# The sample's products over 64 rows made over 128, with zeros in the upper rows

## The chip, the cores and the metric

The kernel runs on one core of a Trainium2 chip. The core has five instruction queues that matter here: TensorE (PE, with its weight loads PEld), VectorE (DVE), ScalarE (ACT), GpSimd (POOL) and SyncE (SP, which issues the DMAs). Each queue runs in the order in which its instructions were written; semaphores hold an instruction back until what it reads is there. The metric is the device time of one execution in microseconds. A profile comes from one further execution.

## The reference

One layer of a streaming encoder for two inputs: a prompt of 2048 new frames, and a sample of 64 frames that continues a running stream. Half of the layer's columns go to attention in chunks (8 heads of 64), the other half to a gated linear recurrence (4 heads of 128). Cut to what matters:

```
xn = rms_norm(h) ; aq, ak, av, ag, hq, hf, hi, hg = split(xn @ w_in)
# attention of the sample: 512 cached keys and its own 64
p = softmax(q @ concat(cache_k, k).T * scale + bias) ; o = p @ concat(cache_v, v)
# recurrence, in blocks, per head (S: 128 x 128)
A = where(mask, q~ @ k~.T, 0) ; o = q~ @ S + A @ v ; S = exp(bl) * S + (k * exp(bl - b)).T @ v
y = h + concat(o_attn * silu(ag), rms_norm(o_rec) * silu(hg)) @ w_out ; rms_norm(y)
```

For the sample the sums over keys (the last 64 of 576) and over frames in a block (64) have 64 terms, where all others have 128.

## The kernel before

All inputs are float32. The prompt is worked through in four stages of 512 frames ("super-blocks"); the second stage has 576 columns, the 64 extra ones being the sample. In each stage PE makes 32 projections of 128 output columns (the products "acc", 24 wide steps each, since operands are split into a high and a low part), and between them the small products of attention and recurrence. The second stage lies at about 260 to 600 us of the span; its projections are cut into 256 and 320 columns.

The tiles that matter: v holds nine blocks of 128 keys for a pair of attention heads; the sample's values are the first 64 rows of block 8. ph holds transposed softmax weights (two buffers). gi (in the code iv) holds the recurrence's values, five blocks of 128 frames, the sample's in block 4. k1 (shown as "k", in the code kn) holds transposed keys. asb (A) holds masked scores. So is the sample's state. wraw serves as the cache's keys and values in this stage.

For the sample three products have 64 rows (frames or keys) on the array's contraction side: in sample_a the last of five products of each head into pv, with ph and v; in rec_block the product kv (kn with iv, "g<-gi,k") and the product og (iv with A, "g<-asb,gi"). There are 4 pairs and 4 recurrent heads. A float32 product is two instructions each with its own weight load, a product of the split type (pv) one.

The order of all five queues is made ahead, when the program is built, by the class Plan. Work is written as threads that yield the time at which they want to go on; Plan keeps a clock for PE and times at which the other engines come free, and charges each instruction by Queue.cost. PE's clock starts each wide product as soon as its operands are there by these estimates, and a thread's small product is put in when its time has come. So an estimate that changes moves rows of the order. The estimate for PE has a part for a change of the array's shape:

```
mode = tuple(next(s for s in (32, 64, 128) if s >= x) for x in (k, m))
extra = 95.0 * (self.plan.mode not in (None, mode))
```

Nearly every instruction is issued through the helper in Queue at line 266, so the profile's rows all show L266, and tiles tell them apart.

Of the kernel before, what the change touches and what calls it, by code (L numbers as in the profile page):

```python
# [17 lines left out]
P = 128  # L18
# [3 lines left out]
DEC = 64  # L22
# [350 lines left out]
def hymba_step(  # L373
# [39 lines left out]
    def T(pool_, shape, dt, tag, **kw):  # L413
        uid[0] += 1
        C.name(homes.get(id(pool_), ""), tag, kw.get("bufs") or 1, f"{tag}_{uid[0]}")
        return pool_.tile(list(shape), dt, tag=tag, name=f"{tag}_{uid[0]}", **kw)
# [13 lines left out]
    def f32(ap):  # L430
        return ap.bitcast(F32)
# [454 lines left out]
    def pair_jobs(sb, p):  # L886
# [10 lines left out]
        def open_():  # L897

            yield from tk["kv"].get()
            d.kd = T(pa, [P, 2, WIN + NMAX], F32R, "kd")  # L900
            d.v = T(pa, [P, 9, 4, 64], F32R, "v")
            d.q = T(pa, [P, 2, QW], F32R, "q")
            if sb:
                cd = carry[sb - 1][p]
                sp.dma_start(f32(d.kd[:, :, 0:512]), cd[:, 0:2, :])
                sp.dma_start(f32(d.v[:, 0:4].rearrange("p t s d -> p (t s d)")),
                             cd[:, 2:4, :].rearrange("p a c -> p (a c)"))
                d.k_t = d.v_t = C.dma(1024)
            C.spawn(load_bias(sb, p, d), 1)
            if smp:  # L910
                C.spawn(sample_cache(d), 1)

        def ev_q(acc, off, bn, t):
# [298 lines left out]
    def sample_cache(d):  # L1212

        p = d.p
        yield from tk["raw"].get()
        yield from tk["raw"].get()
        kc = T(px, [P, 2, 512], F32R, "wraw", bufs=RAWB)
        vc = T(px, [P, 4, 4, 64], F32R, "wraw", bufs=RAWB)
        yield from tk["ck"].get()
        ck = T(wk, [P, 4, P], F32, "ck", bufs=1)  # L1220
        sp.dma_start(ck, cache_k[:, p * P : (p + 1) * P].rearrange("(t q) d -> q t d", q=P))
        t = C.dma(300)
        yield t
        yield from tk["tr"].get()
        pt = tr_ps()
        for j in range(4):
            transpose(pt[:, j * P : (j + 1) * P], ck[:, j, :], ident)
        t = C.pe()
        cv = T(wk, [P, 4, P], F32, "ck", bufs=1)
        sp.dma_start(cv, cache_v[:, p * P : (p + 1) * P].rearrange("(t q) d -> q t d", q=P))  # L1230
        tv = C.dma(300)
        yield "A", t
        yield from split_k(pt, kc, 0, 512, t)
        tk["tr"].put(1, t)
        yield "A", tv
        yield from split_v(cv, vc, 0, 4, P, tv)
        tk["ck"].put()
        d.cache = (kc, vc)

    def sample_a(d, c0, marks):  # L1240
        yield lambda: d.left == 1
        yield lambda: d.cache is not None and d.q_n >= c0 + DEC and d.k_n >= c0 + DEC and d.v_n >= c0 + DEC
        yield "D", max(d.q_t, d.k_t, d.v_t)
        q, kd, v, p = d.q, d.kd, d.v, d.p
        kc, vc = d.cache


        spans = [(kc, 0, 512), (kd, 512 + c0, DEC)]

        z = c0 + DEC  # L1250
        for part in (q, ql):
            dve.memset(f32(part[:, :, z : z + DEC]), 0.0)
            dve.tensor_copy(part[:, 1, z + DEC : z + 2 * DEC], f32(part[:, 1, c0:z]))
        t = C.dve(500)
        yield t
        yield from tk["s_ps"].get()
        yield from tk["pr"].get()
        sps = s_ps()
        for i, (ks, k0, kn) in enumerate(spans):
            for part in (q, ql):  # L1260
                for h in range(2):
                    a = (c0, z)[h]
                    mm(sps[:, i, :kn], part[:, h, a : a + P], ks[:, h, k0 : k0 + kn], kn,
                       start=part is q and h == 0, stop=part is ql and h == 1)
        t = C.pe()
        yield "D", t
        s = T(wk, [P, 640], F32, "pr", bufs=PRB)
        nm = T(wk, [P, 2], F32, "nm", bufs=4)
        for h in range(2):
            hs = own[h]  # L1270
            for i, kn in enumerate((512, DEC)):
                dve.tensor_tensor_reduce(s[hs, i * 512 : i * 512 + kn], sps[hs, i, :kn],
                                         d.bias[hs, h, 64 * h + i * 512 : 64 * h + i * 512 + kn],
                                         1.0, 3e38, ALU.add, ALU.min, nm[hs, i : i + 1])
                t = C.dve(kn, t)
        dve.tensor_tensor(nm[:, 0:1], nm[:, 0:1], nm[:, 1:2], ALU.min)
        t = C.dve(10, t)
        tk["s_ps"].put(1, t)
        d.left -= 1
        if d.left == 0:  # L1280
            tk["bias"].put()
        yield "A", t
        out = []
        yield from softmax_exp(s, nm, 576, out, t)
        pr, t = out[0]
        yield lambda: marks[-1]["pv"] and turn["ph"] == turn["given"]
        yield t + 300.0
        phs = []
        for j0, nj, kr in ((0, 4, P), (4, 1, DEC)):
            yield from tk["tr"].get()  # L1290
            pt = tr_ps()
            for j in range(j0, j0 + nj):
                transpose(pt[:kr, (j - j0) * P : (j - j0 + 1) * P], pr[:, j * P : j * P + kr], ident)
            t = C.pe()
            if j0:
                tk["pr"].put(1, t)
            yield "A", t
            yield from tk["ph"].get()
            ph = T(wk, [P, 2, 512], F32R, "ph", bufs=2)
            t = yield from split_p(pt, ph, kr, nj * P, t)  # L1300
            tk["tr"].put(1, t)
            phs.append(ph)
        yield t + 200.0
        yield from tk["mixa"].get()
        mix = T(wk, [P, 256], F32, "mixa", bufs=2)
        yield from tk["pv"].get()
        pv = psum("pv").rearrange("p (h s q) -> p h s q", h=2, s=2)[:, :, :, :DEC]
        for h in range(2):
            for j in range(5):
                kr = P if j < 4 else DEC  # L1310
                cc = (j % 4) * P + h * DEC
                mm(pv[:, h], vcols(vc, j, h, kr) if j < 4 else vcols(v, 4 + c0 // P, h, kr), phs[j // 4][:kr, :, cc : cc + DEC], P,
                   start=(j == 0), stop=(j == 4))
        tk["ph"].put(2, C.pe())
        t = C.pe()
        yield "A", t
        for h in range(2):
            t = yield from finish_pv(h, pv[:, h], mix, DEC, t)
        tk["pv"].put(1, t)
        tk["raw"].put(2)  # L1320
        C.spawn(mix_out(d, mix, c0, DEC, t, True), 1)
# [5 lines left out]
    def head_jobs(sb, h):  # L1327
# [44 lines left out]
        def ev_i(acc, off, bn, t):  # L1372
            yield from tk["vT"].get()
            yield "A", t
            it = T(wk, [P, 512], F32, "vT", bufs=2)
            act.copy(it[:, :bn], acc)
            t = C.act(bn, t)
            tk["acc"].put(1, t)
            yield lambda: ifree()
            yield t + 300.0  # L1380
            yield from tk["g"].get()
            pt = psum("g")
            full = bn // P
            for j in range((bn + P - 1) // P):
                rr = min(P, bn - j * P)
                transpose(pt[:rr, j * P : (j + 1) * P], it[:, j * P : j * P + rr], ident)
            t = C.pe()
            tk["vT"].put(1, t)
            yield "A", t
            k = off // P  # L1390
            act.copy(r.iv[:, k : k + full, :], pt[:, : full * P].rearrange("p (t d) -> p t d", d=P))
            if bn % P:
                rr = bn % P
                act.copy(r.iv[:rr, k + full, :], pt[:rr, full * P : (full + 1) * P])
            t = C.act(bn, t)
            tk["g"].put(1, t)
            r.i_n += bn
            r.t = max(r.t, t)
# [51 lines left out]
    def rec_block(r, off, bn, lastb):  # L1450
# [136 lines left out]
        yield "A", t  # L1587
        kn = tmp("k1").rearrange("p (c t) -> p c t", t=P)
        for cs, w in merged():
            act.copy(kn[:w, cs], tg[:w, cs])  # L1590
        t = C.act(bn, t)
        yield t + 200.0
        kv = bank()
        iv = r.iv
        for i, (cc, nbk, smp) in enumerate(chunks):
            w = nbk * 32
            mm(kv[:, i], kn[:w, i], iv[:w, (off + cc) // P, :], P, True, start=True, stop=True)
        t = C.pe()
        yield "D", t
        before = []  # L1600
# [28 lines left out]
        og = bank()  # L1629
        for i, (cc, nbk, smp) in enumerate(chunks):  # L1630
            w = nbk * 32
            mm(og[:, i, :w], iv[:w, (off + cc) // P, :], A[:w, i, :w], P, True,
               start=True, stop=before[i] is None)
            if before[i] is not None:
                mm(og[:, i, :w], before[i], qh[:, cc : cc + w], P, True, start=False, stop=True)
# [656 lines left out]
```

## Time and profile before

| | |
|---|---|
| median of 3 runs | 1268.1 us |
| lowest and highest run | 1268.01 and 1269.66 us |
| the profiled execution | 1267.05 us |
| its span, first to last instruction | 1265.3 us |
| granted TensorE clock | 0.999 |
| busy share PE, PEld, DVE, ACT, POOL | 98, 86, 70, 56, 30% |
| HBM traffic | 186.66 MB read, 83.62 MB written |

Rows of a timeline give the start in us from the span's start, the duration of the merged row in us, the engine, the operation and tiles (out<-in), the array's rows*columns for PE, what streams (partitions x elements), the count, and in brackets an idle time ahead with what ended it. Instructions on PE overlap, so starts tell more than durations. A merged row may hide that the last of its instructions have another shape. In a group's row stand busy us, mean ns, and idle time ahead of it.

### The profile page before, as it was taken

How to read it: one execution, taken by the hardware profiler on the slowest of the kernel's cores; microseconds unless marked ns; L12 is line 12 of the kernel's file. 1: busy time of each engine (PE TensorE's matmuls, PEld its weight loads, DVE VectorE, ACT ScalarE, POOL GpSimd, SP SyncE). 2: the span in 40 equal slices, each digit the busy share in tenths (PEclk: the TensorE clock that was granted, in tenths of full speed). 3: DMA queues.
4: the chain of work that ended last, by engine and by line, in shares of the span. 5: the costliest groups of instructions: out<-in, count | busy, mean ns of one | idle time of the engine just before them, and what ended most of it. 6: DMA issues, size and time to landing. Idle time of an engine off the chain costs nothing. (4 is left out here: it accounts for less than half of the span.)

```text
span 1265.3 us, 22177 instructions
## 1 busy us (share of the span) xinstructions
PE 1245.4 (98%) x8120; PEld 1084.0 (86%) x8120; DVE 891.5 (70%) x1854; ACT 707.4 (56%) x1548; POOL 375.2 (30%) x687
## 2 busy tenths in 40 slices
PE   8999999999999999999999999999999999999997
PEld 7788887899999999998888888998888888788786
DVE  6786869766857668687584748784848574578886
ACT  5363546665645557575565656763636454753443
POOL 6766665111110110101634635110101104451110
PEclk9999999999999999999999999999999999999999
DMA  7877777655353464545879597646363657886331
GB/s 258 318 271 248 262 274 279 219 180 199 128 191 127 166 214 157 190 153 193 277 244 313 210 352 257 235 147 234 127 229 117 228 187 272 317 282 207 125 133 67
DMA packets 94830, 271.72 MB, mean 215 GB/s; under 512 B 10305, under 2 KB 43073, under 8 KB 77058
## 3 DMA queue, kind: packets, MB, share of 16 engines
q1 hardware_dynamic: 94722, 270.31, 60.7%
q8 instruction: 64, 1.05, 0.3%
q14 instruction: 44, 0.36, 0.1%
HBM read 186.66 MB, written 83.62 MB: 214 GB/s over the span
## 5 line engine op out<-in xcount | busy, mean ns | idle before, releaser
L266 PE MATMUL acc<-xh,w 128*128 128x512 f32 (+2 forms) x2720 | 567.4, 347 | 1.0 <-ACT sig L266 0.8
L266 PEld LDWEIGHTS acc<-xh,w 128*128 128x128 f32 x2720 | 436.1, 189 | 52.2 <-issue 1.9
L266 PE MATMUL acc<-xl,w 128*128 128x512 f32 (+2 forms) x1360 | 298.0, 348 | 0.0
L266 PEld LDWEIGHTS acc<-xl,w 128*128 128x128 f32 x1360 | 219.6, 189 | 24.8 <-issue 0.5
L266 POOL TENSOR_TENSOR mixa<-mixa,sga 128x256 f32<-128x256 f32 (+1 forms) x36 | 30.2, 840 | 352.1 <-DVE mixa L266 279.9
L266 DVE CUSTOM_DVE_ANT_0 pr<-s,bias 128x640 f32<-128x640 f32 (+5 forms) x144 | 100.7, 703 | 35.3 <-PE s L266 34.8
L266 ACT ACTIVATE pr<-pr,nm 128x640 f32<-128x640 f32 (+4 forms) x132 | 100.8, 763 | 38.2 <-DVE nm L266 37.2
L266 ACT CAST ph<-tr 128x512 fp32r<-128x512 f32 (+3 forms) x176 | 88.1, 508 | 60.1 <-PE tr L266 29.0
L266 POOL TENSOR_TENSOR w<-wraw,w 128x256 fp32r<-128x256 f32 x120 | 105.4, 907 | 48.4 <-DVE w L266 32.7
L266 DVE TENSOR_TENSOR ph<-tr,ph 128x512 fp32r<-128x512 f32 (+3 forms) x176 | 100.9, 589 | 9.4 <-ACT ph L266 8.2
L266 PE MATMUL pv<-ph,v 128*128 128x256 f32 (+2 forms) x344 | 97.5, 373 | 3.1 <-DVE ph L266 2.4
L266 PE MATMUL tr<-ident,pr 128*128 128x128 f32 x580 | 90.8, 273 | 1.8 <-DVE sig L266 0.7
L266 PEld LDWEIGHTS tr<-ident,pr 128*128 128x128 f32 x580 | 70.3, 140 | 16.0 <-issue 3.8
L266 ACT ACTIVATE sig<-acc 128x256 f32<-128x256 f32 (+2 forms) x86 | 42.8, 498 | 72.9 <-PE acc L266 72.6
L266 DVE TENSOR_SCALAR pr<-pr,sm 128x640 f32<-128x640 f32 (+3 forms) x124 | 68.6, 553 | 4.4
L266 DVE TENSOR_TENSOR mixa<-mixa,pv 64x256 f32<-64x256 f32 (+1 forms) x144 | 56.8, 394 | 20.8 <-ACT mixa L266 16.7
L266 ACT COPY vT<-acc 128x512 f32<-128x512 f32 (+2 forms) x64 | 31.2, 488 | 66.6 <-PE acc L266 66.5
L266 PEld LDWEIGHTS pv<-ph,v 128*128 128x128 f32 (+1 forms) x344 | 57.3, 189 | 10.9 <-issue 2.0
L266 ACT ACTIVATE sig<-sig 128x512 f32<-128x512 f32 (+2 forms) x109 | 57.3, 527 | 10.0 <-DVE gk L266 7.3
L266 POOL TENSOR_TENSOR k<-ob 128x512 f32<-128x512 f32 (+2 forms) x20 | 17.8, 891 | 145.4 <-ACT ob L266 145.4
L266 PE MATMUL s<-kd,q 128*128 128x320 f32 (+3 forms) x232 | 56.9, 315 | 0.1
L266 POOL TENSOR_TENSOR xn<-wraw,xn 128x256 fp32r<-128x256 f32 x48 | 37.8, 803 | 61.9 <-ACT xn L266 61.8
(315 smaller groups left out, 2100.7 us busy)
## 6 DMA issues: line engine op xcount, KB each, us to landing
w<-wd SPq DMA_DIRECT2D x96, 1024.0 KB, 5.0
wd<-w SPq DMA_DIRECT2D x32, 1024.0 KB, 7.3
wraw<-in_w_in_dram SPq DMA_DIRECT2D x30, 512.0 KB, 5.4
wod<-xn SPq DMA_DIRECT2D x28, 512.0 KB, 4.2
xn<-in_x_prompt_dram SPq DMA_DIRECT2D x23, 512.0 KB, 5.5
bias<-biasd SPq DMA_DIRECT2D x12, 640.0 KB, 7.1
carry<-kd SPq DMA_DIRECT2D x12, 512.0 KB, 7.9
carry<-v SPq DMA_DIRECT2D x12, 512.0 KB, 5.3
```

Of the source, the lines that this page charges most:

```text
L266: r = f(*args, **kw)
```

## The change

The three products get 128 rows, and memsets on POOL write zeros into the upper 64 rows of their operands: of v's block 8 when a pair's tiles are opened, of ph's first 128 columns, of gi's block 4, and of k1's sample column. A's upper rows are zero already, since A is zeroed at the start and only entries under the mask are written. So per pair and head four memsets are added, 16 in all. The zeros add nothing to the sums.

```diff
@@ pair_jobs, open_
             if smp:
+                pool.memset(f32(d.v[DEC:, 4 + WIN // P]), 0.0)
                 C.spawn(sample_cache(d), 1)
@@ sample_a
             ph = T(wk, [P, 2, 512], F32R, "ph", bufs=2)
+            if kr < P:
+                pool.memset(f32(ph[kr:, :, :P]), 0.0)
             t = yield from split_p(pt, ph, kr, nj * P, t)
...
-                kr = P if j < 4 else DEC
                 cc = (j % 4) * P + h * DEC
-                mm(pv[:, h], vcols(vc, j, h, kr) if j < 4 else vcols(v, 4 + c0 // P, h, kr), phs[j // 4][:kr, :, cc : cc + DEC], P,
+                mm(pv[:, h], vcols(vc, j, h, P) if j < 4 else vcols(v, 4 + c0 // P, h, P), phs[j // 4][:, :, cc : cc + DEC], P,
                    start=(j == 0), stop=(j == 4))
@@ head_jobs, ev_i
                 rr = bn % P
+                pool.memset(r.iv[rr:, k + full, :], 0.0)
                 act.copy(r.iv[:rr, k + full, :], pt[:rr, full * P : (full + 1) * P])
@@ rec_block
         for cs, w in merged():
+            if w < P:
+                pool.memset(kn[w:, cs], 0.0)
             act.copy(kn[:w, cs], tg[:w, cs])
...
-            w = nbk * 32
-            mm(kv[:, i], kn[:w, i], iv[:w, (off + cc) // P, :], P, True, start=True, stop=True)
+            mm(kv[:, i], kn[:, i], iv[:, (off + cc) // P, :], P, True, start=True, stop=True)
...
-            mm(og[:, i, :w], iv[:w, (off + cc) // P, :], A[:w, i, :w], P, True,
+            mm(og[:, i, :w], iv[:, (off + cc) // P, :], A[:, i, :w], P, True,
```

With one shape less, the planner charges less to PE, and rows move. The order differs on PE around three og products (heads 0, 2 and 3), in the scores behind heads 0 and 2, at one block of head 1 and in the first block of the third stage; on DVE and ACT at the same scores, where a row minimum moves ahead of a softmax scaling and a copy of an accumulator ahead of the norm's logarithm; on DVE once more, where a key product moves between the two gate sums of a pair; on SP one weight load passes one store; on POOL there are only the memsets.

PE from the og product of head 0 to the first score product behind it ("s<-kd"; "g<-q,ones" is the norm's sum). Before:

```order
L266 MATMUL g_3675<-asb_10_82,gi_3287 128x64
L266 MATMUL g_3675<-bm_3551,So_3634 128x64
L266 MATMUL acc_3683<-xh_156,w_3345 128x256 x8
L266 MATMUL acc_3683<-xl_157,w_3345 128x256 x8
L266 MATMUL acc_3683<-xh_156,w_3345 128x256 x6
L266 MATMUL g_3724<-q_763_3694,ones_75 128x320
L266 MATMUL acc_3683<-xh_156,w_3345 128x256 x2
L266 MATMUL acc_3732<-xh_156,w_3345 128x320 x8
L266 MATMUL acc_3732<-xl_157,w_3345 128x320 x8
L266 MATMUL acc_3732<-xh_156,w_3345 128x320 x8
L266 MATMUL acc_3766<-xh_156,w_3456 128x256 x2
L266 MATMUL s_3771<-kd_3434,q_3436 128x320 x2
```

And now:

```order
L266 MATMUL acc_3677<-xh_156,w_3345 128x256 x2
L266 MATMUL g_3683<-asb_10_82,gi_3287 128x128
...
L266 MATMUL g_3683<-asb_10_82,gi_3287 128x64
L266 MATMUL g_3683<-bm_3553,So_3637 128x64
L266 MATMUL acc_3677<-xh_156,w_3345 128x256 x6
L266 MATMUL acc_3677<-xl_157,w_3345 128x256 x8
L266 MATMUL acc_3677<-xh_156,w_3345 128x256 x8
L266 MATMUL g_3729<-q_764_3701,ones_75 128x320
L266 MATMUL acc_3732<-xh_156,w_3345 128x320 x8
L266 MATMUL acc_3732<-xl_157,w_3345 128x320 x8
L266 MATMUL acc_3732<-xh_156,w_3345 128x320 x6
L266 MATMUL s_3767<-kd_3435,q_3437 128x320 x2
```

Two wide steps now stand ahead of og, the norm's sum has as many behind og as before, and the first score product comes ahead of four 256-wide and two 320-wide steps that it followed. (The second row of "g<-q,ones" is left out.)

PE at the score products of the recurrence ("g<-q,k") in the first block of the third stage, behind the sample's last pv products. Before:

```order
L266 MATMUL acc_7557<-xh_156,w_7150 128x512 x4
L266 MATMUL acc_7557<-xl_157,w_7150 128x512 x6
L266 MATMUL g_7638<-q_1472_7514,k_1473_7515 32x32
...
L266 MATMUL acc_7557<-xl_157,w_7150 128x512 x2
L266 MATMUL acc_7557<-xh_156,w_7150 128x512 x6
L266 MATMUL g_7681<-ident_69,bl_7630 128x128 x4
```

And now:

```order
L266 MATMUL acc_7573<-xh_156,w_7165 128x512 x4
L266 MATMUL acc_7573<-xl_157,w_7165 128x512 x4
L266 MATMUL g_7651<-q_1472_7529,k_1473_7530 32x32
...
L266 MATMUL acc_7573<-xl_157,w_7165 128x512 x4
L266 MATMUL acc_7573<-xh_156,w_7165 128x512 x4
L266 MATMUL g_7695<-ident_69,bl_7645 128x128 x4
```

The score products come two 512-wide steps sooner.

POOL between a gate product of a head and the small factors of its next block, second head. Before:

```order
L266 TENSOR_TENSOR k_901_4418<-ob_4414 128x256
L266 TENSOR_TENSOR ob_4414<-ob_4414,gg_4461 128x256
L266 MEMSET pf_4550 128x16
L266 MEMSET sf_4551 128x16
L266 MEMSET fq_4553 128x8
```

And now:

```order
L266 TENSOR_TENSOR k_902_4426<-ob_4422 128x256
L266 MEMSET gi_4317 64x128
L266 TENSOR_TENSOR ob_4422<-ob_4422,gg_4466 128x256
L266 MEMSET v_4510 64x256
L266 MEMSET pf_4558 128x16
```

The fills of gi and v stand around the gate product, ahead of the factors.

## The prediction

> **What bounds the kernel now.** I read the page's busy shares first, then the sums of the stretch in which the sample's 64 rows are handled (260 to 600 us), then TensorE's groups by shape, and then the order in time around the products that the change touches.
>
> ```profile
> PE 1245.4 (98%) x8120; PEld 1084.0 (86%) x8120; DVE 891.5 (70%) x1854; ACT 707.4 (56%) x1548; POOL 375.2 (30%) x687
> ```
> ```profile
> sum 340.00, PE 338.19 PEld 323.25 DVE 238.22 ACT 203.85 POOL 45.00; mean PE 84.55 PEld 80.81 DVE 59.56 ACT 50.96 POOL 11.25
> ```
>
> TensorE (PE) is busy 98% of the span and 338.19 of the 340 us of the stretch; DVE has 238, ACT 204, POOL 45. So the time here is the sum of PE's steps: a step that gets shorter shortens the run, unless PE arrives somewhere before its input and stands. Idle POOL time is worth nothing by itself.
>
> The products concerned are these, in the groups by shape (rows*columns of the array, then partitions x elements that stream):
>
> ```profile
> L266 PE MATMUL pv<-ph,v 64*128 64x128 f32 x8 | 2.6, 324 | 0.0
> L266 PE MATMUL g<-gi,k 64*128 64x128 f32 x8 | 1.9, 322 | 0.0
> L266 PE MATMUL g<-asb,gi 64*128 64x64 f32 x8 | 1.7, 296 | 0.0
> ```
>
> They are 24 instructions of 8120: two products per pair of attention heads (pv), and per recurrent head one key-value product (kv, "g<-gi,k") and one output product (og, "g<-asb,gi"), these two as two instructions each. Their busy time of 6.2 us tells little, since matmuls overlap; what counts is the step from one start to the next. How such a stretch runs when every product has 128 rows:
>
> ```profile
> 356.88 0.39 PE L266 MATMUL g<-bm,stp 128*128 128x128 f32 x2
> 357.10 0.39 PE L266 MATMUL g<-asb,gi 128*128 128x128 f32 x2
> 357.33 0.39 PE L266 MATMUL g<-bm,S 128*128 128x128 f32 x2
> 357.47 0.96 PE L266 MATMUL acc<-xh,w 128*128 128x256 f32 x6
> ```
>
> A pair of instructions takes 0.22 us from start to start, so 0.11 a step; the last pair before a wide product shows 0.14. The same program text with the 64-row pair in it:
>
> ```profile
> 303.00 0.39 PE L266 MATMUL g<-bm,S 128*128 128x128 f32 x2
> 303.32 0.43 PE L266 MATMUL g<-asb,gi 64*128 64x64 f32 x2
> 303.68 0.43 PE L266 MATMUL g<-bm,So 128*128 128x64 f32 x2
> 303.92 0.48 PE L266 MATMUL acc<-xh,w 128*128 128x256 f32 x2
> ```
>
> The pair ahead of the 64-row one takes 0.32, the 64-row pair 0.36, the pair behind it 0.24: 0.92 us from 303.00 to 303.92. PE has no recorded wait there (idle 0.0 in the groups above). PE pays when the row shape changes, on the way in and on the way out, though half of the array's rows do no work.
>
> **The change part by part.**
>
> *og.* With 128 rows I give the three pairs 0.22 + 0.23 + 0.14 = 0.59 (the row shape of 356.88 to 357.47). The pair with 64 streamed columns may be a little shorter, not longer. Gain 0.92 - 0.59 = 0.33 us, four heads: 1.32.
>
> *kv.* Six instructions with the 64-row pair at their end, and four of 128 rows elsewhere, each with what follows:
>
> ```profile
> 297.29 1.02 PE L266 MATMUL g<-gi,k 128*128 128x128 f32 x6
> 298.24 1.91 PE L266 MATMUL acc<-xh,w 128*128 128x256 f32 x12
> ```
> ```profile
> 509.61 0.60 PE L266 MATMUL g<-gi,k 128*128 128x128 f32 x4
> 509.97 0.70 PE L266 MATMUL pv<-ph,v 128*128 128x512 f32 x2
> ```
>
> Six took 0.95; four took 0.36, and two more at 0.11 make 0.58. Gain 0.37, four heads: 1.48. (The row's merged label hides that its last two have 64 rows.)
>
> *pv.* Here every group of four 128-row products is followed by one of 64 rows, twice per pair:
>
> ```profile
> 349.92 0.38 PE L266 MATMUL g<-ident,vT 128*128 128x128 f32 x2
> 350.06 0.83 PE L266 MATMUL acc<-xh,w 128*128 128x320 f32 x4
> ...
> 351.71 0.66 PE L266 MATMUL pv<-ph,wraw 128*128 128x128 f32 x4
> 352.30 0.32 PE L266 MATMUL pv<-ph,v 64*128 64x128 f32 x1
> 352.55 0.66 PE L266 MATMUL pv<-ph,wraw 128*128 128x128 f32 x4
> 353.15 0.32 PE L266 MATMUL pv<-ph,v 64*128 64x128 f32 x1
> 353.40 0.44 PE L266 MATMUL g<-ident,bl 128*128 128x128 f32 x2
> 353.59 1.13 PE L266 MATMUL acc<-xl,w 128*128 128x320 f32 x6
> ```
>
> The 64-row ones take 0.25 each instead of 0.11 (0.28 for both), the four between them 0.60 instead of 0.44 (0.16), the two transposes behind 0.19 instead of the 0.14 of 349.92 (0.05). The first four took 0.59, but part of that comes from the narrow products ahead; I take 0.10 of it, the 0.32 against 0.22 at og's entry. Sum 0.59 per pair, four pairs: 2.36. All together 1.32 + 1.48 + 2.36 = 5.16 us of PE time. The ends: 4.6, if the wide product behind still needs a longer step, and 5.4.
>
> One rule of the Trainium skill speaks against this. "TensorEngine Tiling (Array Packing)", sections Theoretical Speedup and When to Use Tiling, advises two row tiles where the contraction has 64 rows and promises up to twice the speed. By it the 24 products would be the faster form now, the change would double their steps, and the time would be 1271.7 where the rows give 1263.9. The rows above do not bear that out: nothing runs in the other 64 rows, and the steps are longer, not shorter.
>
> *The sixteen memsets* (64 partitions of 128 or 256 elements) go to POOL. The nearest row is a fill of 128x128:
>
> ```profile
> masks.py:197 POOL MEMSET ident<- 128x128 f32 x1 | 0.2, 204 | 0.3 <-POOLq L2279 0.3
> ```
>
> At 0.2 to 0.4 us each they add about 5 us to POOL's 45 in 340, off the path. What could put them on it is POOL's order: the fill of v stands ahead of the small factors pf to fk that DVE needs for a head's second block. The tightest place:
>
> ```profile
> 364.76 0.19 POOL L266 COPY pf<-eb 128x2 f32<-128x2 f32 x1 [0.58 <-ACT eb L266]
> 366.52 0.19 POOL L266 COPY fk<-eb 128x2 f32<-128x2 f32 x1
> ...
> 367.90 0.28 DVE L266 TENSOR_TENSOR q<-q,fq 128x128 f32<-128x128 f32 x1
> ```
>
> POOL waits 0.58 for ACT there, so a fill of 0.3 disappears, and the factors are ready 1.2 us before DVE uses them: cost 0. The fill of ph waits for the ordinary pair's last pv, as ACT's cast into the same buffer does already; behind it stand a gate product and once the square "k<-ob", which wait for work of about that time. The fills of gi and k stand where POOL next waits for ACT. PE's new waits for POOL (kv, pv) are met by then. On SP one weight load passes one store of "ob": cost 0, the store's reader being the out-projection, and the buffer's next writer coming a whole block later.
>
> *The moved rows.* The planner now believes PE to be earlier, so some small products stand a few wide steps sooner, and PE may get there too soon. These are the losses.
>
> Scores of heads 0 and 2: the first one now comes ahead of four 256-wide and two 320-wide steps that stood before it. Its input is DVE's kd:
>
> ```profile
> 308.34 1.34 PE L266 MATMUL acc<-xl,w 128*128 128x320 f32 x8
> 308.89 1.54 DVE L266 TENSOR_TENSOR kd<-vT,kd 64x256 fp32r<-64x256 f32 x2
> 309.51 1.57 PE L266 MATMUL acc<-xh,w 128*128 128x320 f32 x10
> 310.92 0.46 PE L266 MATMUL s<-kd,q 128*128 128x320 f32 x2
> ```
>
> Eight 320-wide steps take 1.17 us, 0.146 each; the six steps are at most 0.88, with the narrower ones about 0.77. kd is done at 310.43, 0.49 before the score. ACT's copy of the accumulator moves ahead of the norm's logarithm, which brings kd perhaps 0.1 sooner. So PE stands 0.77 - 0.49 - 0.1 = 0.2 at the first score, and I add 0.1 for the following ones, where DVE's row minimum moves ahead of a softmax scaling and so nearly keeps up: 0.3 a head, 0.6 in all. Ends: 0, and 0.39 at each of four scores (3.1 for two heads).
>
> og of head 3: its new state waits for a DMA that PE does not bring forward.
>
> ```profile
> 535.33 0.35 DVE L266 SCALAR_TENSOR_TENSOR So<-So,et,g 128x128 f32<-128x128 f32 x1 [0.53 <-DMA So<-in_state_hgrn_dram]
> 535.78 0.45 PE L266 MATMUL g<-asb,gi 128*128 128x128 f32 x2
> ```
>
> og starts right after it. PE now comes 0.37 earlier by kv, less the two 256-wide steps put ahead (about 0.24): loss 0.13. Ends 0 and 0.37 at each of four heads (1.5).
>
> Score products of the next stage's first head ("g<-q,k"): two 512-wide steps less ahead of them.
>
> ```profile
> 592.90 1.55 PE L266 MATMUL acc<-xl,w 128*128 128x512 f32 x6
> 594.18 0.41 DVE L266 TENSOR_TENSOR k<-k,fk 128x256 f32<-128x256 f32 x1
> 594.38 1.28 PE L266 MATMUL g<-q,k 128*32 128x32 f32 x64
> ```
>
> Six steps take 1.48, so two about 0.49, and k was only just in time. DVE now does k's product between two gate sums that wait for ACT, which wins some of it back: loss 0.25, ends 0 and 0.49.
>
> Losses 0.6 + 0.13 + 0.25 = 0.98. Net gain 5.16 - 0.98 = 4.2 us. Later stages keep their order and hang on PE, so they move up whole. The profiled execution took 1267.05 (span 1265.3), so 1262.9; the median of the runs is 1268.1, 1.05 above it: 1263.9.
>
> **The rivals.** *The waits eat it.* All losses at their upper ends: 3.1 + 1.5 + 0.49 = 5.1, and the time is 1268.0. For it: kd, So and k are each in time by half a microsecond or less. Against it: only the first score jumps six steps; the later ones follow DVE's and ACT's own new order, and So of the other heads does not start from a DMA wait right ahead of og.
>
> *POOL's queue, slower.* The fill of v is held behind the old v's users, and with it the factors pf to fk and DVE's products. Suppose it is ordered behind the load into the same tile:
>
> ```profile
> 364.92 0.46 SPq L266 DMA_DIRECT2D v<-carry  x1
> ```
> ```profile
> v<-carry SPq DMA_DIRECT2D x12, 512.0 KB, 6.0
> ```
>
> It would end at 370.9 and start the factors 6.4 us late; less the 1.2 in hand that is 5.2 a head, 20.8 for four, 1284.8. It decides above 1.2 + 4.2/4 = 2.3 us of delay a head. Against it: the fill's rows are not those that the load writes, and the old v's last reader is the pv at 353.15, eleven microseconds ahead.
>
> *The change doesn't do what it says.* The long steps belong to the operands (a short product after long ones), not to the row count, and stay. Then only the losses remain: 1269.1, within 0.2%. Against it: three products with different operands and types show the same price at entry (0.10) and the pair "g<-bm,So", of the same 64 streamed columns and 128 rows, has 0.24.
>
> *The 64-row form is the faster one.* If the 24 steps of 0.11 double and nothing else changes, 2.6 us more and the losses: 1271.7. The Trainium skill's advice named above is this case. Against it stands every row above.
>
> **How the numbers follow.** Forecast as worked out 0.80, with its own range 1262.6 (5.4 gained, no loss) to 1265.5 (4.6 gained, twice the losses); the waits eat it 0.08; POOL's queue 0.05; the steps stay 0.04; 64 rows faster 0.03. 0.2% is 2.5 us, about what a measurement of this kernel can tell from no change. Faster 0.81 (the forecast, and a little of the partly eaten gain), same 0.11, slower 0.08. The range for 8 in 10 is 1262.2 to 1266.6: below, the forecast's end less a little for the runs' scatter (1268.01 to 1269.66); above, part of the way to the first rival.
>
> **What would show it.** The profile after should have no 64-row products but the eight transposes of the sample's input; kv's six in about 0.58 us, og's last pairs at 0.22, pv's ten steps at 0.11; PE's busy time down by about 5 and its idle time up by about 1, at the scores, at og of head 3 and at "g<-q,k". PE waiting for POOL at pv or kv, or POOL's pf waiting for its own fill, would mean that I misjudged the queue; unchanged steps around the three products, that I misread the price.

## The result and the profile after

| | before | after |
|---|---|---|
| median (lowest to highest), us | 1268.01 (1265.58 to 1270.75), 7 runs | 1262.85 (1260.86 to 1263.75), 7 runs |
| the profiled execution, us | 1267.05 | 1260.86 |
| span, us | 1265.3 | 1259.0 |

The ratio is 0.9965 with a 95% interval of 0.9953 to 0.9977: the kernel is 2.9 to 6.0 us faster. The page of the profile after has the same 8120 products and 16 more instructions on POOL:

```profile
PE 1238.8 (98%) x8120; PEld 1081.6 (86%) x8120; DVE 891.9 (71%) x1854; ACT 706.9 (56%) x1548; POOL 379.9 (30%) x703
```

PE is still the bound, and the 16 fills cost POOL 4.7 us of busy time (375.2 to 379.9). The span is 6.3 us shorter, but not all of that is the change. The first work on the sample's input starts 2.0 us earlier in the profile after (255.49 against 257.49 us), in a part of the program that the change doesn't touch. So the comparisons of traces below use one stretch, from the start of the second stage's first "g<-gi,k" product to that of the third stage's second head. It takes 383.02 us before and 378.60 after, a difference of **-4.42 us**.

Now the three products. A timeline of PE after, with kv's six instructions, then og's last three pairs:

```profile
295.28 0.83 PE L266 MATMUL g<-gi,k 128*128 128x128 f32 x6
295.87 1.30 PE L266 MATMUL acc<-xh,w 128*128 128x256 f32 x8
```
```profile
300.84 0.39 PE L266 MATMUL g<-bm,S 128*128 128x128 f32 x2
301.07 0.33 PE L266 MATMUL g<-asb,gi 128*128 128x64 f32 x2
301.24 0.39 PE L266 MATMUL g<-bm,So 128*128 128x64 f32 x2
301.43 0.96 PE L266 MATMUL acc<-xh,w 128*128 128x256 f32 x6
```

kv's six take 0.59 us where they took 0.95, og's pairs 0.23 + 0.17 + 0.19 = 0.59 where they took 0.92. The two groups of pv of one pair of heads:

```profile
349.30 0.66 PE L266 MATMUL pv<-ph,wraw 128*128 128x128 f32 x4
349.80 0.28 PE L266 MATMUL pv<-ph,v 128*128 128x128 f32 x1
349.91 0.61 PE L266 MATMUL pv<-ph,wraw 128*128 128x128 f32 x4
350.36 0.27 PE L266 MATMUL pv<-ph,v 128*128 128x128 f32 x1
350.47 0.51 PE L266 MATMUL acc<-xl,w 128*128 128x320 f32 x2
```

Nine of the ten steps are 0.11 to 0.115 us long and the first, behind the narrow products, 0.16: 1.17 from 349.30 to 350.47, where before took 1.69. In POOL's groups the fills have the length that the prediction gave them:

```profile
L266 POOL MEMSET v<- 64x256 f32 x4 | 1.2, 307 | 0.2
L266 POOL MEMSET ph<- 64x256 f32 x4 | 1.2, 307 | 24.0 <-PE pv L266 23.9
```

The fills of ph wait 6 us each for the pv products that still read the buffer; that is idle POOL time, and no product of PE waits for POOL in this stretch, as PE's waits from 255 to 640 us show (in all, times, longest):

```profile
PE tr L266 <- DVE sig L266: 0.7, 2, 0.4
PE g L266 <- DVE xl L266: 0.4, 2, 0.3
PE g L266 <- ACT gi L266: 0.3, 1, 0.3
PE g L266 <- DVE k L266: 0.3, 1, 0.3
```

The first two were there before, and of the third 0.2. The fourth and the rest of the third belong to what was given back. The scores behind head 0, PE and DVE:

```profile
309.51 0.46 PE L266 MATMUL s<-kd,q 128*128 128x320 f32 x2
309.81 0.45 PE L266 MATMUL s<-kd,ql 128*128 128x320 f32 x2
310.10 0.27 PE L266 MATMUL tr<-ident,vT 128*64 128x128 f32 x1
310.13 1.20 PE L266 MATMUL acc<-xl,w 128*128 128x256 f32 x8
311.16 0.64 PE L266 MATMUL acc<-xh,w 128*128 128x256 f32 x4
311.92 0.53 PE L266 MATMUL s<-kd,q 128*128 128x320 f32 x2
```
```profile
310.94 0.82 DVE L266 CUSTOM_DVE_ANT_0 pr<-s,bias 128x640 f32<-128x640 f32 x1
```

Four 256-wide steps at 0.12 bring PE to 311.64, but the third score starts at 311.92: the one accumulator for scores is free when DVE's row minimum of the second score ends at 311.76. DVE comes to it late because the kd product ahead of it in its queue waited 0.41 for ACT. PE loses 0.28 there and 0.30 at head 2. The list of waits doesn't name it; the gap shows only in the starts. The score products of the third stage, and the recurrence's score products behind the second pair's pv:

```profile
587.15 0.33 PE L266 MATMUL g<-q,k 128*32 128x32 f32 x12
587.77 1.01 PE L266 MATMUL g<-q,k 128*32 128x64 f32 x52 [0.30 <-DVE k L266]
```
```profile
427.25 0.66 PE L266 MATMUL g<-q,k 128*32 128x32 f32 x32 [0.34 <-ACT gi L266]
```

The first stands 0.30 for DVE's k and loses 0.36 against before; the second waited 0.22 before, and 0.34 now.

### The profile page after: what moved, and what is told of

Same layout as the page of the kernel before. It is cut to its first block, busy times and chain, and to the rows that moved or that the text cites. A ratio compares the mean times of both kernels' runs of the same rounds, so it can differ in the third digit from the quotient of the medians.

```text
span 1259.0 us, 22201 instructions
## 1 busy us (share of the span) xinstructions
PE 1238.8 (98%) x8120; PEld 1081.6 (86%) x8120; DVE 891.9 (71%) x1854; ACT 706.9 (56%) x1548; POOL 379.9 (30%) x703
## 5 line engine op out<-in xcount | busy, mean ns | idle before, releaser
L266 PEld LDWEIGHTS pv<-ph,v 128*128 128x128 f32 x344 | 57.4, 190 | 10.3 <-issue 2.0
L266 PE MATMUL s<-kd,ql 128*128 128x320 f32 (+3 forms) x232 | 55.6, 309 | 0.0
```

What stands on the lines that cost most here:

```text
L266: r = f(*args, **kw)
```

## The experiments

Two kinds of numbers are used. The timed ratio is to the kernel before on the same chip. The stretch is that of the profiled execution, given as the difference to the 383.02 us of before; it leaves out the start-up, but is one execution.

**The change once more**, beside the experiments:

> The changed kernel again, beside the kernel before on the same chip, as the measure for the runs next to it. Stretch: from the start of the sample stage's first key-value product (279 us) to that of the third stage's second head (662 us), which the first profile of the change shows 4.4 us shorter than before. Every theory expects 4.3 to 4.5 us less in the stretch and 0.3 to 0.4% less in the whole.

Measured: 1262.08 us against 1266.85, ratio 0.9963 (0.9950 to 0.9976); stretch -4.09. The result holds, and one profile differs from the next by 0.3 us.

**The longer products alone, in the order of before.** The planner is told that the three products still have 64 rows, and the fills aren't charged, so that each engine's queue keeps the order of before:

```diff
+            k = self.plan.rows or k
...
-            mm(kv[:, i], kn[:, i], iv[:, ...], P, True, start=True, stop=True)
+            mm(kv[:, i], kn[:, i], iv[:, ...], P, True, start=True, stop=True, rows=64 if smp else None)
...
-                pool.memset(kn[w:, cs], 0.0)
+                nc.gpsimd.memset(kn[w:, cs], 0.0)
```

(pv, og and the other fills likewise; the first line stands ahead of the planner's "mode".)

> The whole change, but the planner still charges the three products as 64-row ones and nothing for the memsets, so that PE, DVE, ACT and SP keep the order of before. Theory (the price lies in the change of row shape, 5.16 us, and the moved rows give 0.98 of it back): the stretch is 5.0 to 5.4 us shorter than before, 0.6 to 1.0 shorter than with the change as made, and PE does not wait at the scores. Rival (PE waits there because it is early at all, wherever the rows stand): 4.2 to 4.6 us, as with the change as made.

Measured: 1262.36 us, ratio 0.9967 (0.9957 to 0.9977); stretch -3.17. That lies outside both expectations. Since the order is that of before, the two traces can be laid beside each other instruction by instruction: the steps around the products are shorter by 0.39 us a visit for kv (0.34 at the second head), 0.33 for og and 0.56 a pair for pv, together 1.50 + 1.33 + 2.24 = **5.07 us**. What takes 1.9 of it back is mostly one late load, here in DVE's and PE's timelines:

```profile
532.83 0.35 DVE L267 SCALAR_TENSOR_TENSOR So<-So,et,g 128x128 f32<-128x128 f32 x1 [1.77 <-DMA So<-in_state_hgrn_dram]
```
```profile
533.23 0.49 PE L267 MATMUL g<-asb,gi 128*128 128x128 f32 x2 [1.04 <-DVE So L267]
```

The sample's state for head 3 came late, and og lost 1.2 us; a load of cached keys cost 0.47 more. Three waits that were there before are longer by 0.13 each, since PE comes sooner and the operand doesn't (ACT's k and gi, and DVE's k in the third stage). In return og of head 1 doesn't lose the 0.22 that it lost in the profile of before.

**The zeros alone, and the zeros with the new order.** One kernel writes the zeros in the order of before and leaves the products at 64 rows. The other writes them too and leaves the products at 64 rows, but the planner is told 128, which gives the order of after. For kv, against the changed kernel:

```diff
-            mm(kv[:, i], kn[:, i], iv[:, ...], P, True, start=True, stop=True)
+            w = nbk * 32
+            mm(kv[:, i], kn[:w, i], iv[:w, ...], P, True, start=True, stop=True)
```
```diff
+            mm(kv[:, i], kn[:w, i], iv[:w, ...], P, True, start=True, stop=True, rows=128 if smp else None)
```

> The sixteen memsets alone, with the products over 64 rows and the order of before. Theory (POOL is off the path): the stretch within 0.1 us of before, POOL's busy time 4 to 5 us up. Rival (the fills hold up POOL's queue, and DVE and PE behind it): 0.5 us or more longer.

Measured: 1265.86 us, ratio 0.9991 (0.9981 to 1.0000); stretch -0.23. That is more than the 0.1 expected. In the profile of before og of head 1 starts 0.22 late behind its state's load, and here it doesn't; all else sums to 0.01. So **-0.23 is the ground** for the one-part kernels below, and the zeros cost nothing. POOL's busy time from 260 to 600 us is 49.39, up from 45.00:

```profile
sum 340.00, PE 338.16 PEld 323.07 DVE 238.28 ACT 203.76 POOL 49.39; mean PE 338.16 PEld 323.07 DVE 238.28 ACT 203.76 POOL 49.39
```

> The memsets and the order of the changed kernel, row for row on every queue, but the products over 64 rows. Theory (the moved rows only cost): nothing gained, 0 to 0.9 us longer in the stretch than before; less than 0.9 if PE, which is later without the shorter steps, finds the inputs there. Rival (the gain came from the new order): 2 us or more shorter.

Measured: 1266.63 us, ratio 0.9997 (0.9989 to 1.0006); stretch +0.33. The order gives no gain; in the profile it costs 0.56 against the ground, which has the same zeros. The timed intervals of the two overlap.

**One product at a time**, with the order of before and the planner's hint as above; the other two products stay at 64 rows.

> Only the pv product over 128 rows, with all memsets, in the order of before. Theory (0.59 us a pair): the stretch 2.36 us shorter than before (2.2 to 2.5). Rival (the long steps belong to the operands): 0.

> Only the key-value product over 128 rows, with all memsets, in the order of before. Theory (0.37 us a head, and og of two heads then waits for the new state): 1.0 to 1.5 us shorter in the stretch. Rival (operands): 0.

> Only the og product over 128 rows, with all memsets, in the order of before. Theory (0.33 us a head): 1.3 us shorter in the stretch (1.1 to 1.4). Rival (operands): 0.

Measured, one execution each (1267.12 us for the kernel before beside them):

| longer alone | us | stretch | against the ground | steps alone, four visits |
|---|---|---|---|---|
| pv | 1263.18 | -1.75 | -1.52 | -2.24 |
| kv | 1265.66 | -0.60 | -0.37 | -1.50 |
| og | 1262.57 | -1.57 | -1.34 | -1.33 |

The steps are there in each. og keeps its whole gain; pv and kv fall short of what was expected. Against the ground pv gives back 0.72: 0.40 in the same three waits, each 0.13 longer, and 0.23 at og of head 3, where the state had not landed; 0.1 I could not place. The 1.13 that kv gives back is the same load, at og of heads 1 (0.55) and 2 (0.65), which PE reaches sooner. PE at head 1:

```profile
376.54 0.49 PE L267 MATMUL g<-asb,gi 128*128 128x128 f32 x2 [0.28 <-DVE So L267]
```

**What the price belongs to.** In the kernel before, kv's products of a head are six instructions of which the last two have 64 rows. One kernel gives all six 64 rows, the other the first and the last pair:

```diff
+            x = DEC if any(c[2] for c in chunks) else w
-            mm(kv[:, i], kn[:w, i], iv[:w, ...], P, True, start=True, stop=True)
+            mm(kv[:, i], kn[:x, i], iv[:x, ...], P, True, rows=w, start=True, stop=True)
```
```diff
+            x = DEC if any(c[2] for c in chunks) and i != 1 else w
```

> The kernel before, in its order, with all three key-value products of the blocks that hold the sample over 64 rows (six instructions in place of two; the upper 64 frames of the other two products are left out of the sum). Theory (the price is paid per change of row shape, of which there are as many as before): kv takes 0.95 us a head as before, the stretch changes by less than 0.2 us. Rival (the price is paid per 64-row instruction, 0.37 us for two): 0.74 us a head more, 2.9 us in the stretch.

> The kernel before, in its order, with the first and the third of these key-value products over 64 rows and the one between them over 128 (the upper 64 frames of the first are left out). Theory (price per change: four changes of shape in place of two): 0.3 to 0.4 us a head more, 1.2 to 1.6 us longer in the stretch. Rival (no price for a change): 0.

PE's timeline at the first head, all six and then in turns (a merged row takes the shape of its first instruction):

```profile
297.11 0.93 PE L267 MATMUL g<-gi,k 64*128 64x128 f32 x6
297.97 1.76 PE L267 MATMUL acc<-xh,w 128*128 128x256 f32 x11
```
```profile
298.02 1.32 PE L267 MATMUL g<-gi,k 64*128 64x128 f32 x6
299.27 1.90 PE L267 MATMUL acc<-xh,w 128*128 128x256 f32 x12
```

Six at 64 rows take 0.86 us, where two of six took 0.95: the change of shape has moved ahead of the first of them, where PE's step has grown from 0.12 to 0.21, and three times as many 64-row products cost no more. The stretch is -0.37, so -0.15 against the ground (1266.55 us). In turns they take 1.25: a second change on the way in and out costs 0.39 on this visit. The stretch is +1.30, 1.53 above the ground, for four visits 0.38 each (1269.13 us; the kernel before beside it 1264.98). So the price is paid **per change of row shape**, in and out, not per product of 64 rows.

**POOL's queue.** To try the rival in which POOL holds the second block's factors back, the fill of v is made fourteen times over, in the order of before:

```diff
-                nc.gpsimd.memset(f32(d.v[DEC:, 4 + WIN // P]), 0.0)
+                for _ in range(14):
+                    nc.gpsimd.memset(f32(d.v[DEC:, 4 + WIN // P]), 0.0)
```

> The whole change in the order of before, with the fill of v written fourteen times in place of once, so that POOL comes about 4 us later to the factors pf to fk. Theory (POOL has 1 to 3 us in hand there, and beyond that PE waits at the recurrence's scores): 1 to 4 us longer in the stretch than with one fill. Rival (POOL is off the path however late it is): 0.

Measured: 1270.55 us (the kernel before beside it 1264.98), stretch +3.33, 6.5 above the same kernel with single fills (the first experiment). That was more than expected. POOL, PE and DVE in order of time, and PE's sum of waits:

```profile
363.23 5.04 POOL L916 MEMSET v<- 64x256 f32 x14
368.09 0.33 PE L267 MATMUL g<-q,k 128*32 128x32 f32 x12
370.25 0.18 POOL L267 COPY fk<-eb 128x2 f32<-128x2 f32 x1
370.56 0.29 DVE L267 TENSOR_TENSOR k<-k,fk 128x128 f32<-128x128 f32 x1
370.90 0.30 PE L267 MATMUL g<-q,k 128*32 128x64 f32 x7 [2.49 <-DVE k L267]
```
```profile
PE g L267 <- DVE k L267: 6.0, 4, 2.5
```

The chain runs as the rival has it: fill, factors, DVE's product, PE's scores. The thirteen more fills take 4.7 us a head, but for a part of that POOL would have waited for ACT's eb. Counted against PE's own place, the factor fk, the last that DVE's k product needs, comes 3.0, 4.6, 2.7 and 3.5 us later than with single fills, and PE loses 1.27, 2.67, 1.0 and 1.75, 6.7 in all. So 1.75 to 1.9 us of each head's delay stay without cost; a single fill of 0.3 is far inside.

Two more terms stand in the 6.5. Behind the 2.7 us that PE stood at the second head, its 320-wide steps took 0.267 us in place of 0.147, with a granted clock of 0.56 from 371.4 to 375.1 us; that cost another 1.5. Behind the three shorter stands the clock stayed at 1.00. And the late loads, 1.8 us in the first experiment, cost nothing here.

**The state's load, earlier.** In both orders, SP issues the load of the sample's state at the start of the head's block and not where its use is planned:

```diff
+        if bn % P:
+            so = [T(pg, [P, P], F32, "So", bufs=2) for _ in range(2)]
+            nc.sync.dma_start(so[0], state_in[h])
...
-                old, new = (T(pg, [P, P], F32, "So", bufs=2) for _ in range(2))
-                sp.dma_start(old, state_in[h])
+                old, new = so
...
```

> The changed kernel, with the load of the sample's recurrent state put at the start of its block on SP, about ten us sooner; PE, DVE, ACT and POOL keep the change's order. Theory (the steps gain 5.06 us and 0.22 of a wait for that load; the moved rows take 0.5 to 0.6 back at the scores and three waits of 0.13 the rest): the stretch is 4.3 to 4.6 us shorter than before, with no wait for the state at og. Rival (the moved rows cost nothing, what is missing is the load): 5.0 or more.

> The whole change in the order of before, with the same earlier load. Theory (in that order only the late loads, 1.2 and 0.4 us, kept the gain at 3.2; three waits of 0.13 stay): 4.7 to 5.0 us shorter in the stretch than before, 0.3 to 0.5 shorter than with the change's order, and the whole 0.3 to 0.45% faster than before. Rival (the old order is the worse one for a PE that is early): about 3.2 again, with other waits in the place of the load's.

Measured (the kernel before beside them 1266.54 us): order of after 1261.55 us, ratio 0.9961 (0.9947 to 0.9975), stretch -4.39; order of before 1261.56 us, ratio 0.9962 (0.9950 to 0.9975), stretch -4.76. Both stretches are as expected. With the order of before, DVE's and PE's timelines at head 3, where 1.2 us were lost above, now read:

```profile
530.64 0.35 DVE L267 SCALAR_TENSOR_TENSOR So<-So,et,g 128x128 f32<-128x128 f32 x1
531.58 0.38 PE L267 MATMUL g<-asb,gi 128*128 128x128 f32 x2
```

DVE no longer waits for a DMA. The order of before is then 0.37 better in the profile, and not at all in the timed runs; neither is better than the change beyond the intervals.

## Why the prediction was right

It said 1263.9 us, faster, and 1262.85 came. By its own steps, over the stretch:

| step | predicted, us | measured, us |
|---|---|---|
| og, four heads | -1.32 | -1.33 |
| kv, four heads | -1.48 | -1.50 |
| pv, four pairs | -2.36 | -2.24 |
| sum of the steps | -5.16 | -5.07 |
| scores of heads 0 and 2 | +0.6 | +0.28 + 0.30 |
| og of head 3 | +0.13 | -0.06 |
| third stage, "g<-q,k" | +0.25 | +0.36 |
| "g<-q,k" behind the second pair's pv | not seen | +0.13 |
| a wait of "g<-gi,k" near 355 us that went away | not seen | -0.14 |
| og of head 1: late load in the profile of before | not seen | -0.22 |
| net | -4.2 | -4.42 |
| fills on POOL, the load on SP | 0 | 0 |

*The price of a change of shape* was read off the starts before, and og and kv are within 0.02 us and pv within 0.12 for four visits. The guess that 0.10 of the first four pv products' 0.59 belongs to the entry holds: they take 0.50 now. The rival by which 64 rows are the faster form is refuted by the first experiment, and so is the one by which the steps stay. No kernel here ran two 64-row products side by side, so what that would give stays open. Two sums of the prediction are off by 0.1 (1268.1 - 5.4 is 1262.7, and 1263.9 + 20.8 is 1284.7); nothing hangs on them.

*The scores* lost what was said, but not where. The first score was put 0.2 behind DVE's kd, with 0.1 for those that follow. In the trace after, the first score starts at 307.68, right behind its six 320-wide steps from 306.80 on (0.147 each), so PE loses nothing there; kd is just in time:

```profile
306.29 1.44 DVE L266 TENSOR_TENSOR kd<-vT,kd 64x256 fp32r<-64x256 f32 x2
```

The loss is at the third score, which needs the accumulator that DVE's row minimum frees. The step "DVE's row minimum moves ahead of a softmax scaling and so nearly keeps up" had it the wrong way about: it was the tight place, and cost 0.28 and 0.30 where 0.1 was given. That the sum fits is luck.

*og of head 3* was a misreading of a varying quantity as a fixed one. DVE waited for the state's load again, but og came 0.23 behind DVE's product, where before it came 0.10 behind, so PE lost nothing:

```profile
529.61 0.35 DVE L266 SCALAR_TENSOR_TENSOR So<-So,et,g 128x128 f32<-128x128 f32 x1 [0.62 <-DMA So<-in_state_hgrn_dram]
530.19 0.38 PE L266 MATMUL g<-asb,gi 128*128 128x128 f32 x2
```

Which of the four heads loses, and how much, changes from profile to profile. Against steps without a wait it is 0.22 at head 1 and 0.06 at head 3 before; none here; 0.37 at head 1 in the change's second profile; 1.3 at head 3 in the first experiment; 0.55 and 0.65 at heads 1 and 2 with kv alone. With the load issued early, none loses. The term should have been a range over four heads, as its upper end was, and not 0.13 at one.

*POOL's queue* was rightly put at nothing, but its rival was priced too high. The prediction took 1.2 us a head as all the slack and let the gain be gone at 2.3. With the measured delays of 3.0, 4.6, 2.7 and 3.5 us that rule gives 9 us; PE stood 6.7, since 1.75 to 1.9 us a head cost nothing. The 1.2 was the distance to DVE's q product, and PE needs DVE's results later than that.

What stays open: the timed runs can't tell the predicted 4.2 from 5.2, the difference of the medians, and whether the moved rows cost the 0.4 to 0.6 us that the profiles show, or nothing.

## What to carry to other kernels

Where a PE-bound kernel has single short products among full ones, read their price from start to start, from the full product ahead to the one behind, and compare with the same program text without the short one; the instruction's own time and the group's idle time don't show it. Where the upper rows can be kept at zero by an engine with slack, the full shape is cheaper, and where they can't, put the short products side by side, so that the shape changes once. When PE gains a few tenths at many places, list what is only just in time there, the DMAs among it: one load issued where it is needed took 1.2 of 5.1 us in a profile here.

## What the runs showed of the hardware

*Among themselves 64-row products are as fast as 128-row ones.* With all six of kv at 64 rows, the steps inside the run are 0.11 us, as they are at 128.

*A change to 64 columns has no such price, one to 32 has.* The transpose at 310.10 above (128*64) stands among products of 128*128, and the next one starts 0.03 us behind it, as it does behind a transpose of 128*128 that stands ahead of a wide product. Wide products of 128*64 step at 0.23 us, as those of 128*128 do. But the step ahead of the recurrence's score products (128*32) is longer by 0.09 us in both kernels wherever no wait adds to it: 0.24 in place of 0.15 for a 320-wide step, 0.21 in place of 0.12 for a 256-wide one, 0.32 in place of 0.23 for a 512-wide one. So it is not the row side alone that costs.

*The price shows in the weight loads.* The loads around og's 64-row pair before, and the same ones after:

```profile
302.89 0.30 PEld L266 LDWEIGHTS g<-bm,S 128*128 128x128 f32 x2
303.32 0.29 PEld L266 LDWEIGHTS g<-asb,gi 64*128 64x128 f32 x2
303.68 0.30 PEld L266 LDWEIGHTS g<-bm,So 128*128 128x128 f32 x2
303.89 0.42 PEld L266 LDWEIGHTS acc<-xh,w 128*128 128x128 f32 x3
```
```profile
300.74 0.30 PEld L266 LDWEIGHTS g<-bm,S 128*128 128x128 f32 x2
300.96 0.30 PEld L266 LDWEIGHTS g<-asb,gi 128*128 128x128 f32 x2
301.18 0.30 PEld L266 LDWEIGHTS g<-bm,So 128*128 128x128 f32 x2
```

After, each pair of loads begins 0.08 us before the pair ahead has ended. Before, the 64-row pair begins 0.13 after the end of the one ahead, and the 128-row pair behind it 0.07 after; behind that the overlap is back. The Trainium skill ("TensorE: Matmul & The Clock Gate", section The mechanism) says that a weight load overlaps running products only when its row group differs; in the same section it also lets a load into a background weight buffer be pulled ahead. The trace does not agree with the first: the load at 300.96 has the same 128 rows as the products "g<-bm,S", which start at 300.84 and 300.95 and run to 301.23, and it is at the change of rows that the overlap is missing. It fits the second, which no run here tells apart from other reasons. Why the array waits at the change, no run shows.

*A load of 64 KB has no fixed time.* From issue to landing the sample's four states took 3.3 to 5.9 us before, 2.9 to 6.7 in the first experiment, 2.9 to 5.6 after, and 1.9 to 9.0 when they were issued early in the order of after. One such load cost 1.2 us in a single profile, and two profiles differed by 2.0 us before the sample's work began; the span of a single profile is no measure of a change of this size.
